# Six merge gates of branch B, in pairs of seven half-width products

## The chip, the core and the metric

The kernel runs on one core of a Trainium2 chip, as one program with one launch. The core has five engines that work side by side, each through its own queue in order: TensorE (PE) multiplies matrices and transposes into PSUM; VectorE (DVE) and ScalarE (ACT) work element by element and read PSUM; GpSimd (POOL) works element by element in SBUF; SyncE (SP) issues nearly all DMA. An engine that waits for a semaphore holds up everything behind it in its queue. The metric is the device time of one execution in microseconds (us), the median of three runs.

## The reference

Two layers of a bidirectional encoder, 512 tokens of width 1024, all in float32:

```python
h = x @ w_in[l]
c_q, c_kv, k_r, gate_a, q_d, k_d, v_d, gate_b, gates = _split_cols(h)
# branch A: latent attention, 8 heads -> y_a (512 wide), y_a = (o_a * silu(gate_a)) @ w_branch_a[l]
# branch B: differential attention, 4 heads, each head's output RMS-normed -> y_b,
#           y_b = (o_b * silu(gate_b)) @ w_branch_b[l]
g = jax.nn.sigmoid(gates + b_merge[l])
merged = g[..., :D_MODEL] * y_a + g[..., D_MODEL:] * y_b
out = merged @ w_out[l]
x = _layer_norm(DEEPNORM_ALPHA * x + out, ln_gamma[l], ln_beta[l])
```

The change is about the second half of `gates`, 1024 columns of `x @ w_in` in 8 chunks of 128 columns (gtB0 to gtB7).

## The kernel before

**Layout and precision.** x stands feature-major in SBUF: 8 chunks of 128 features by 512 tokens. Every float32 operand is split into a high and a low part that PE multiplies at full speed: xH and xL for x, `slot` (L107 to L114) for a weight: one load of 128x1024 into a `wr` tile (2 buffers), one cast on ACT (L110), two subtractions on DVE (L113). A product is three matmuls, high x high, high x low, low x high (`mm3`, L123 to L126). `proj` (L128) makes one chunk of 128 output columns: 8 feature chunks x 3 = 24 matmuls of 512 tokens.

**Stages of a layer.** Latent projections, then branch A's heads, then branch B's four heads, then gates and branch outputs, the merge, the output projection and the LayerNorm. While one head's values are worked out, the next head's scores and other projections are woven in (`dfill`, L567). `diff_values` (L455) of a branch B head: transposes of the probabilities (L179) into PSUM, a cast (L181, ACT) and a low part (L182, DVE) per chunk, 3 value matmuls per chunk, a copy (L467), transposes (L473), squares (L476), two small DVE operations (L478, L479), the power -0.5 on POOL (L481), a broadcast by four transposes (L141) and three DVE operations (L484, L485, L161) that give yB. The last head (3) has no next head beside it. `yB` is needed by `branch(1, c)` (12 matmuls of 512 for one chunk), `yA`, held in 8 `y` tiles, by `branch(0, c)`, whose last call is chunk 7 (m7). After head 3: gate B0, then four times two gates and two branch products, each merged on DVE (L596, L597) and split (L163, L164) into `qm` tiles.

**What sets the order.** The code says what depends on what, in program order, with a number of buffers per tag; a scheduler then sets every engine's queue by its own estimate of when each operand is ready. It may move a matmul of a later projection between two steps of an earlier chain, if its weights are there by its estimate. At run time each queue keeps that order.

Of the kernel before, what the change touches and what calls it, by code (L numbers as in the profile page):

```python
# [11 lines left out]
F32 = mybir.dt.float32  # L12
# [6 lines left out]
DM = 1024  # L19
SEQ = 512  # L20
P = 128
# [21 lines left out]
    + [f"o{n}{k}" for n in range(2) for k in range(4)]  # L43
)

# [5 lines left out]
def hybrid_trunk(ctx: ExitStack, tc: tile.TileContext, x, xT, wlat, wts, prm, dlam, gb, tab, rtab, out):  # L51
# [23 lines left out]
    def pt_(tag):  # L75
        return ps.tile([P, 512], F32, tag=tag, name=nm("ps" + tag), bufs=PB[tag])
# [106 lines left out]
        return h, lo  # L183

    def layer(l, last):
        pr = prms[:, l, :]
        A, B = slice(0, 64), slice(64, 128)

# [266 lines left out]
        def diff_values(h, pts, v, g, s1):  # L455
# [22 lines left out]
            nc.vector.scalar_tensor_tensor(e, s1, EPS_DIFF, s1, ALU.mult, ALU.mult)  # L478
            nc.vector.scalar_tensor_tensor(e, ss, 1.0 / 128, e, ALU.mult, ALU.add)  # L479
            r = small(4)  # L480
            nc.gpsimd.tensor_tensor(r, e, mhalf[:, 0:4], ALU.pow)  # L481
            yield
            b = bcast(r)
            nc.vector.scalar_tensor_tensor(g, b, gsc, g, ALU.mult, ALU.mult)  # L484
# [7 lines left out]
        def branch(which, c, ys):  # L492
            if c % 2 == 0:
                br[which] = slot(l, f"br{'AB'[which]}{c // 2}")
            bhh, bll = br[which]
            acc = pt_("acc")
            for k in range(4):
                o = ((c % 2) * 4 + k) * P
                mm3(acc, bhh[:, o:o + P], bll[:, o:o + P], ys[k][0], ys[k][1], k == 0, k == 3)
            return acc  # L500

        def gate(which, c):
            acc = proj(l, f"gt{'AB'[which]}{c}")
            th = t2("tmp")
            col = which * 8 + c
            nc.scalar.activation(th, acc, AF.Tanh, bias=bh[:, col:col + 1], scale=0.5)
            return th

        mA = []

# [18 lines left out]
                        gens.remove(g)  # L529
            return r  # L530

        qd, kd, vd, gB, hold = {}, {}, {}, {}, {}

        def run(names):
            for f in names:
                i = int(f[-1])
                if f[0] == "a":
                    gateA(i)
                elif f[0] == "g":
                    hold[i] = gate(0, i)  # L540
                elif f[0] == "m":
                    mergeA(i, hold.pop(i))
                elif f[0] == "v":
                    vd[i] = diff_v(i)
                elif f[0] == "b":
                    gB[i] = silu2(proj(l, f"gb{i}"))
                elif f[0] == "q":
                    qd[i] = diff_q(i)
                elif f[0] == "k":
                    kd[i] = diff_k(i)  # L550
# [5 lines left out]
        for h in range(8):  # L556
# [8 lines left out]
            run(fill[h])  # L565
        run(["b0", "v0"])
        dfill = {  # L567
            0: ["g0", "m0", "g1", "m1", "b1", "q2", "k2", "g2", "m2", "g3", "m3"],
            1: ["v1", "b2", "q3", "k3", "g4", "m4", "g5", "m5"],
            2: ["b3", "g6", "m6", "g7", "m7"],  # L570
            3: [],
        }
        s1 = {h: small(4, "s1", 3) for h in range(4)}
# [13 lines left out]
        hold["B0"] = gate(1, 0)  # L587
        next(tail)
        merged = []
        for c2 in range(4):  # L590
            ths = [gate(1, 2 * c2) if c2 else hold.pop("B0"), gate(1, 2 * c2 + 1)]
            for i in range(2):
                c = 2 * c2 + i
                acc = branch(1, c, yB)
                th = ths[i]
                nc.vector.scalar_tensor_tensor(th, th, 1.0, acc, ALU.add, ALU.mult)  # L596
                nc.vector.tensor_tensor(th, th, mA[c // 2][:, i * 512:i * 512 + 512], ALU.add)  # L597
                merged.append(split(th, "qm", 0.5))


        src = x if l == 0 else xs
# [85 lines left out]
def _pack(i, l):  # L687
# [2 lines left out]
    outs = []  # L690
    for s in SLOTS:
        c = int(s[-1]) if s[-1].isdigit() else 0
        if s.startswith("vd"):
            a = _fm(w_in, O_VD + int(s[2]) * 256 + r(256))[:, 4 * c:4 * c + 4]
        elif s[:2] in ("ga", "qd", "kd", "gb"):
# [83 lines left out]
```

## Time and profile before

| | |
|---|---|
| time, median of 3 runs (range) | 855.28 us (854.16 to 855.56) |
| profiled execution | 854.49 us, span 852.7 us |
| PE busy | 841.5 us (99%), 4121 matmuls |
| DVE, ACT, POOL busy | 587.5, 428.8, 22.7 us |
| DMA read from HBM, written | 70.80 MB, 4.19 MB |
| granted PE clock | 0.998 |

In the profile a row of a group reads: line, engine, operation, output<-input by the program's names, shapes, count | busy us, mean ns of one | idle us of the engine just before them, and what ended most of it. A timeline row reads: start us, length us, engine, line, operation, output<-input, shape, count, and in brackets the idle time before it with what ended it. A row of a window reads: stretch, its length, then the busy time and number of instructions of PE, of its weight loads (PEld), DVE, ACT, POOL, then granted clock, DMA share and GB/s. A DMA row reads: output<-input, queue, count, KB each, median us from issue to landing.

### The profile page before, as it was taken

How to read it: one execution, taken by the hardware profiler on the slowest of the kernel's cores; microseconds unless marked ns; L12 is line 12 of the kernel's file. 1: busy time of each engine (PE TensorE's matmuls, PEld its weight loads, DVE VectorE, ACT ScalarE, POOL GpSimd, SP SyncE). 2: the span in 40 equal slices, each digit the busy share in tenths (PEclk: the TensorE clock that was granted, in tenths of full speed). 3: DMA queues.
4: the chain of work that ended last, by engine and by line, in shares of the span. 5: the costliest groups of instructions: out<-in, count | busy, mean ns of one | idle time of the engine just before them, and what ended most of it. 6: DMA issues, size and time to landing. Idle time of an engine off the chain costs nothing.

```text
span 852.7 us, 11036 instructions
## 1 busy us (share of the span) xinstructions
PE 841.5 (99%) x4121; PEld 694.6 (81%) x4121; DVE 587.5 (69%) x1066; ACT 428.8 (50%) x843; POOL 22.7 (3%) x30
## 2 busy tenths in 40 slices
PE   9999999999999999999999999999999999999996
PEld 8777877878898888888897778788788888888885
DVE  6789988586656745455867899877667566545457
ACT  5767775463534633332336777755546354433310
POOL 0100000000000000000120000000000000000001
PEclk9999999999999999999999999999999999999999
DMA  8411111213222352323532110122222233433322
GB/s 295 126 44 33 37 50 50 74 31 102 91 74 75 123 173 83 94 96 118 184 107 69 42 37 26 50 52 73 75 75 75 81 94 123 157 97 94 98 75 98
DMA packets 27701, 75.70 MB, mean 89 GB/s; under 512 B 3200, under 2 KB 7808, under 8 KB 27648
## 3 DMA queue, kind: packets, MB, share of 16 engines
q1 hardware_dynamic: 27648, 75.01, 27.8%
q8 instruction: 32, 0.52, 0.3%
q14 instruction: 21, 0.17, 0.1%
HBM read 70.80 MB, written 4.19 MB: 88 GB/s over the span
## 4 chain that ended last, share of the span: by engine, by line
PE 94%; ACT 3%; DVE 2%; issue 0%; POOL 0%; DVEq 0%
PE psacc L124 23%; PE psacc L125 23%; PE psacc L126 23%; PE pstr L179 4%; PE pspv L362 2%; PE pspv L124 2%; PE pssc L124 2%; PE pssc L125 2%; PE pssc L126 2%; PE pspv L363 2%; PE pspv L125 2%; PE pspv L126 2%; ACT wh L110 1%; PE pssc L441 1%; PE pssc L445 1%; PE pssc L446 1%
## 5 line engine op out<-in xcount | busy, mean ns | idle before, releaser
L113 DVE TENSOR_TENSOR wl<-wr,wh 128x512 fp32r<-128x512 f32 x192 | 127.1, 685 | 146.8 <-ACT wh L110 146.4
L124 PE MATMUL psacc<-xH,wh 128*128 128x512 f32 x512 | 201.6, 394 | 0.0
L125 PE MATMUL psacc<-xL,wh 128*128 128x512 f32 x512 | 200.8, 392 | 0.0
L126 PE MATMUL psacc<-xH,wl 128*128 128x512 f32 x512 | 200.4, 391 | 0.0
L110 ACT CAST wh<-wr 128x1024 fp32r<-128x1024 f32 x96 | 100.8, 1050 | 176.8 <-PE psacc L125 119.0
L124 PEld LDWEIGHTS psacc<-xH,wh 128*128 128x128 f32 x512 | 96.2, 188 | 19.7
L126 PEld LDWEIGHTS psacc<-xH,wl 128*128 128x128 f32 x512 | 96.2, 188 | 19.2
L125 PEld LDWEIGHTS psacc<-xL,wh 128*128 128x128 f32 x512 | 96.2, 188 | 19.2
L172 ACT ACTIVATE p<-pssc,sm 128x512 f32<-128x512 f32 x128 | 88.2, 690 | 27.1 <-DVE sm L170 26.5
L170 DVE TENSOR_REDUCE sm<-pssc 128x1 f32<-128x512 f32 x128 | 86.6, 682 | 5.0 <-PE pssc L126 2.8
L181 ACT CAST pt<-pstr 128x512 fp32r<-128x512 f32 x96 | 55.7, 586 | 28.8 <-PE pstr L179 28.6
L182 DVE TENSOR_TENSOR pt<-pstr,pt 128x512 fp32r<-128x512 f32 x96 | 64.7, 684 | 7.2 <-ACT pt L181 6.3
L179 PE MATMUL pstr<-ident,p 128*128 128x128 f32 x384 | 57.3, 272 | 0.0
L179 PEld LDWEIGHTS pstr<-ident,p 128*128 128x128 f32 x384 | 47.3, 140 | 12.0 <-ACT p L172 0.5
L125 PE MATMUL psacc<-wl,xH 128*128 128x256 f32 x128 | 36.3, 284 | 0.0
L124 PE MATMUL psacc<-wh,xH 128*128 128x256 f32 x128 | 36.3, 284 | 0.0
L126 PE MATMUL psacc<-wh,xL 128*128 128x256 f32 x128 | 36.2, 283 | 0.0
L362 PE MATMUL pspv<-pt,vs 128*128 128x512 f32 x64 | 29.3, 458 | 0.3
L124 PE MATMUL pssc<-kv,qm 128*128 128x512 f32 x64 | 26.8, 423 | 0.5 <-ACT kv L303 0.5
L124 PE MATMUL psacc<-y,wh 128*128 128x512 f32 x64 | 25.8, 403 | 0.0
L363 PE MATMUL pspv<-pt,vs 128*128 128x512 f32 x64 | 25.5, 398 | 0.0
L125 PE MATMUL pssc<-kv,qm 128*128 128x512 f32 x64 | 25.4, 397 | 0.0
(287 smaller groups left out, 1559.0 us busy)
## 6 DMA issues: line engine op xcount, KB each, us to landing
wr<-in_wts_dram SPq DMA_DIRECT2D x106, 512.0 KB, 3.5
p<-in_xT_dram SPq DMA_DIRECT2D x8, 256.0 KB, 5.3
qr<-in_wts_dram SPq DMA_DIRECT2D x16, 128.0 KB, 2.1
p<-in_gb_dram SPq DMA_DIRECT2D x8, 256.0 KB, 3.0
y<-in_x_dram SPq DMA_DIRECT2D x8, 256.0 KB, 5.6
x_scratch<-y SPq DMA_DIRECT2D x8, 256.0 KB, 2.1
y<-x_scratch SPq DMA_DIRECT2D x8, 256.0 KB, 5.0
out_dram<-y SPq DMA_DIRECT2D x8, 256.0 KB, 2.0
```

The lines of the kernel that those rows point to most:

```text
L110: nc.scalar.copy(hi, raw)
L113: nc.vector.tensor_tensor(lo[:, c], raw[:, c], fr(hi[:, c]), ALU.subtract)
L124: nc.tensor.matmul(o, lhsT=lh, rhs=rh, start=start, stop=False)
L125: nc.tensor.matmul(o, lhsT=lh, rhs=rl, start=False, stop=False)
L126: nc.tensor.matmul(o, lhsT=ll, rhs=rh, start=False, stop=stop)
L170: nc.vector.tensor_reduce(m, S, axis=AX.X, op=ALU.max, negate=True)
L172: nc.scalar.activation(p, S, AF.Exp, bias=m, scale=1.0, accum_out=sums)
L179: nc.tensor.transpose(b[:, t * P:(t + 1) * P], pts[t][:, c * P:(c + 1) * P], ident)
L181: nc.scalar.copy(h, b)
L182: nc.vector.tensor_tensor(lo, b, fr(h), ALU.subtract)
L362: nc.tensor.matmul(pv, lhsT=v, rhs=ph, start=kc == 0, stop=False)
L363: nc.tensor.matmul(pv, lhsT=v, rhs=pl, start=False, stop=kc == NT - 1)
```

## The change

Of the 8 gates of branch B in a layer, gtB2 to gtB7 are made as three pairs (`gate_pair`). A pair is a product of a weight of 1024 x 256 and x of 1024 x 512. Each is seen as 2 x 2 blocks: weight blocks of 512 features x 128 columns (r11, r12, r21, r22), x blocks of 512 features x 256 tokens. Instead of 8 block products it makes 7 (a form of Strassen's scheme), each 4 feature chunks x 3 = 12 matmuls of 256 tokens: 84 matmuls where two gates had 48 of 512.

The sums of weight blocks (four adds of 128x512 a pair) are made on POOL (L553) in `kv` tiles; the 7 weight operands are split into high and low parts by ACT and DVE (L558, L559). The raw weights come as four loads of 256 KB into `p` tiles (L548), not through `wr`. The sums of x blocks (`x_forms`, L520) are the same for all pairs of a layer: per j two adds of 128x512 and four of 128x256 on POOL, in `qm` tiles, written to DRAM by two DMAs from POOL's queue; each of the four sums is read back by one load into a `wr` tile and split into four `y` tiles (sums 0 and 1) or `qm` tiles (`load_x_form`, L532). Products add up in three PSUM tiles (Y, Z, X) of half width; between products ACT copies them out (L598 to L606) and DVE adds. The weight blocks and results are the same numbers in another order of sums; rounding differs.

Also changed: the branch products of B use the `sc` PSUM tiles; pairs stand ahead of the branch chunks 0, 2 and 4 in the program; the slots of the weights in DRAM are in another order, with a pair's two gates side by side. The x sums stand in `dfill` behind the power of head 0 (x0, x1) and of head 1 (x2, x3), the read-backs (y0 to y3) behind m7.

```diff
-    + ["gtB0", "gtB1", "brB0", "gtB2", "gtB3", "brB1", "gtB4", "gtB5", "brB2", "gtB6", "gtB7", "brB3"]
+    + ["gtB0", "gtB1", "brB0", "brB1", "brB2", "brB3"] + [f"gtB{c}" for c in range(2, 8)]
...
+        xf = dram.tile([P, 4, 1024], F32, name=f"xf{l}")
...
-            nc.gpsimd.tensor_tensor(r, e, mhalf[:, 0:4], ALU.pow)
+            pows[h] = nc.gpsimd.tensor_tensor(r, e, mhalf[:, 0:4], ALU.pow)
...
-            acc = pt_("acc")
+            acc = pt_("sc" if which else "acc")
...
+        c1, c2 = slice(0, 256), slice(256, 512)
+        XF = []
+        def x_forms(j):
+            ra, rb, f, g = (t2("qm") for _ in range(4))
+            for v, k in ((ra, j), (rb, j + 4)):
+                nc.gpsimd.tensor_tensor(v, fr(xH[:, k, :]), fr(xL[:, k, :]), ALU.add)
+            nc.gpsimd.tensor_tensor(f[:, c1], ra[:, c1], ra[:, c2], ALU.subtract)
+            nc.gpsimd.tensor_tensor(f[:, c2], f[:, c1], rb[:, c2], ALU.add)
+            nc.gpsimd.tensor_tensor(g[:, c1], rb[:, c2], ra[:, c2], ALU.subtract)
+            nc.gpsimd.tensor_tensor(g[:, c2], f[:, c2], rb[:, c1], ALU.subtract)
+            for i, v in ((0, f), (2, g)):
+                nc.gpsimd.dma_start(xf[:, i:i + 2, j * 256:(j + 1) * 256], v.rearrange("p (a b) -> p a b", a=2))
+        def load_x_form(i):
+            raw = load(xf[:, i, :])
+            out = []
+            for o in (0, 512):
+                h, lo = split(raw[:, o:o + 512], "y" if i < 2 else "qm", -1.0 if i == 1 else None)
+                out += [(h[:, c], lo[:, c]) for c in (c1, c2)]
+            XF.append(out)
+        def gate_pair(c):
+            i = SLOTS.index(f"gtB{c}")
+            G = wts[l, i:i + 2].rearrange("s (q r) n -> (s q) (r n)", r=2)
+            raw = []
+            for i in range(4):
+                raw.append(t2("p"))
+                nc.sync.dma_start(raw[i], G[:, i * 512:(i + 1) * 512])
+            r11, r12, r21, r22 = raw
...
+            f3 = add(r11, r21)
+            f1 = add(r21, r22)
+            f2 = add(f3, r22)
+            f4 = add(f2, r12)
+            a, b = halves()
+            W11 = form(r11, a)
+            F1 = form(f1, b)
+            a, b = halves()
+            F2 = form(f2, a)
+            F4 = form(f4, b)
+            F3 = form(f3, two("op"))
+            W12 = form(r12, two("pt"))
+            W22 = form(r22, two("pt"))
...
+            def product(o, w, xs_, first):
+                for k in range(4):
+                    (wh, wl), (h, lo) = (v[:, k * P:(k + 1) * P] for v in w), xs_[k]
+                    for n, (a, b) in enumerate(((wh, h), (wh, lo), (wl, h))):
+                        nc.tensor.matmul(o, lhsT=a, rhs=b, start=first and k == 0 and n == 0,
+                                         stop=k == 3 and n == 2, skip_group_check=True)
+            tag = "g" if c == 4 else "qw"
+            t0, t1 = t2(tag), t2(tag)
+            Y, Z, X = (pt_("acc")[:, c1] for _ in range(3))
+            product(Y, W11, block(0, 0), True)
+            nc.scalar.copy(t0[:, c1], Y)
+            product(Z, F1, XF[0], True)
+            nc.scalar.copy(t1[:, c1], Z)
+            product(Y, F2, XF[1], False)
+            nc.scalar.copy(t0[:, c2], Y)
+            product(Z, F4, block(1, 1), False)
+            nc.vector.tensor_tensor(t0[:, c2], Z, t0[:, c2], ALU.add)
+            product(Y, F3, XF[2], False)
+            nc.scalar.copy(t1[:, c2], Y)
+            product(X, W12, block(1, 0), True)
+            nc.vector.tensor_tensor(t0[:, c1], X, t0[:, c1], ALU.add)
+            nc.vector.tensor_tensor(t1[:, c2], t1[:, c2], t1[:, c1], ALU.add)
+            col = 8 + c
+            nc.scalar.activation(t0, t0, AF.Tanh, bias=bh[:, col:col + 1], scale=0.5)
+            product(Y, W22, XF[3], False)
+            nc.scalar.activation(t1[:, c2], t1[:, c2], AF.Tanh, bias=bh[:, col + 1:col + 2], scale=-0.5)
+            nc.scalar.activation(t1[:, c1], Y, AF.Tanh, bias=bh[:, col + 1:col + 2], scale=-0.5)
+            return t0, t1
...
+                elif f[0] == "x":
+                    with tc.issue_after(pows[max(pows)].ins):
+                        x_forms(i)
+                elif f[0] == "y":
+                    load_x_form(i)
...
-            0: ["g0", "m0", "g1", "m1", "b1", "q2", "k2", "g2", "m2", "g3", "m3"],
-            1: ["v1", "b2", "q3", "k3", "g4", "m4", "g5", "m5"],
-            2: ["b3", "g6", "m6", "g7", "m7"],
+            0: ["x0", "x1", "g0", "m0", "g1", "m1", "b1", "q2", "k2", "g2", "m2", "g3", "m3"],
+            1: ["x2", "x3", "v1", "b2", "q3", "k3", "g4", "m4", "g5", "m5"],
+            2: ["b3", "g6", "m6", "g7", "m7", "y0", "y1", "y2", "y3"],
...
-        for c2 in range(4):
-            ths = [gate(1, 2 * c2) if c2 else hold.pop("B0"), gate(1, 2 * c2 + 1)]
...
+        ths = [hold.pop("B0"), gate(1, 1)]
+        for c in range(8):
+            if c in (0, 2, 4):
+                ths += gate_pair(c + 2)
+            acc = branch(1, c, yB)
```

The order of the queues changes at head 3 of branch B. First PE, in layer 0, around the end of head 3's values. Before, `pspv_3129` are its value matmuls, `psacc_3213` is gate gtB0, L473 its transposes; fourteen more rows of `psacc_3213` follow, then L141 on `pstr_3240`, then gate gtB1:

```order
L124 MATMUL pspv_3129<-pt_3168,kv_2601 128x512
L125 MATMUL pspv_3129<-pt_3169,kv_2601 128x512
L126 MATMUL pspv_3129<-pt_3168,kv_2602 128x512
L124 MATMUL psacc_3213<-xH,wh_3208 128x512
L125 MATMUL psacc_3213<-xL,wh_3208 128x512
L126 MATMUL psacc_3213<-xH,wl_3209 128x512
L124 MATMUL psacc_3213<-xH,wh_3208 128x512
L473 MATMUL pstr_3192<-ident,op_3188 128x128 x4
L125 MATMUL psacc_3213<-xL,wh_3208 128x512
```

And with the change, where `pspv_3218` are the value matmuls, `pstr_3329` is the broadcast of the power (L141) and `psacc_3302` is gtB0:

```order
L141 MATMUL pstr_3264<-ident,sm_3036 128x128 x4
L124 MATMUL pspv_3218<-pt_3257,kv_2650 128x512
L125 MATMUL pspv_3218<-pt_3258,kv_2650 128x512
L126 MATMUL pspv_3218<-pt_3257,kv_2651 128x512
L474 MATMUL pstr_3281<-ident,op_3277 128x128 x4
L141 MATMUL pstr_3329<-ident,sm_3293 128x128 x4
L124 MATMUL psacc_3302<-xH,wh_3297 128x512
L125 MATMUL psacc_3302<-xL,wh_3297 128x512
L126 MATMUL psacc_3302<-xH,wl_3298 128x512
```

The 24 matmuls of gtB0 stood between and behind the steps of head 3's values, all ahead of the last broadcast; now all of them stand behind it, and nothing else stands between the steps.

Second, SP's queue, in layer 0. Before, from gtA6's weights: `wr_3059` is brA3, `wr_3081` gtA7, `wr_3206` gtB0:

```order
L104 DMA wr_3025<-in_wts_dram 128x1024
L104 DMA wr_3059<-in_wts_dram 128x1024
L104 DMA wr_3081<-in_wts_dram 128x1024
L104 DMA wr_3206<-in_wts_dram 128x1024
L610 DMA p_3684<-in_gb_dram 128x512
```

With the change, behind gtA7's weights: the four loads from `xf_90` are the x sums 0 to 3, `p` are blocks of pairs' weights, `wr_3295` is gtB0:

```order
L104 DMA wr_3178<-xf_90 128x1024
L548 DMA p_3373<-in_wts_dram 128x512
L548 DMA p_3375<-in_wts_dram 128x512
L548 DMA p_3377<-in_wts_dram 128x512
L548 DMA p_3379<-in_wts_dram 128x512
L104 DMA wr_3188<-xf_90 128x1024
L548 DMA p_3557<-in_wts_dram 128x512
L104 DMA wr_3198<-xf_90 128x1024
L104 DMA wr_3208<-xf_90 128x1024
L548 DMA p_3559<-in_wts_dram 128x512
L548 DMA p_3561<-in_wts_dram 128x512
L104 DMA wr_3295<-in_wts_dram 128x1024
```

gtB0's weights followed gtA7's at once; now four x sums and seven weight blocks stand ahead of them. `wr_3295` takes the buffer of `wr_3198`, which is free when sum 2 is split.

Third, DVE with the change, behind the squares of head 3 (L480 is the second small operation, L485 the first that reads the broadcast, `wl_3298` the low part of gtB0's weights):

```order
L480 SCALAR_TENSOR_TENSOR sm_3290<-sm_3280,sm_3290 128x4
L161 TENSOR_TENSOR lat_3271<-op_3020,lat_3271 128x512
L485 SCALAR_TENSOR_TENSOR g_3072<-pstr_3329,gs_477,g_3072 128x512
L113 TENSOR_TENSOR wl_3298<-wr_3295,wh_3297 128x512 x2
L486 TENSOR_TENSOR op_3277<-op_3277,g_3072 128x512
```

The low part of gtB0's weights stood ahead of head 3's first L182 in DVE's queue; now it stands behind an operation that reads the broadcast. Layer 1 has the same orders at these places. On POOL the power of head 3 now stands behind five weight adds.

More of the change, by code (lines that the diff above doesn't have):

```diff
@@ new lines, in load_x_form, with add, form, halves @@
+        def load_x_form(i):
[13 more added lines that the diff above has]
+            r11, r12, r21, r22 = raw
+            def add(a, b):
+                o = t2("kv")
+                nc.gpsimd.tensor_tensor(o, a, b, ALU.add)
+                return o
+            def form(v, room):
+                hi, lo = room
+                nc.scalar.copy(hi, v)
+                nc.vector.tensor_tensor(lo, v, fr(hi), ALU.subtract)
+                return room
+            def halves():
+                h, lo = t2("wh", F32R, 1024), t2("wl", F32R, 1024)
+                return [(h[:, o:o + 512], lo[:, o:o + 512]) for o in (0, 512)]
+            def two(tag):
+                return t2(tag, F32R), t2(tag, F32R)
+            f3 = add(r11, r21)
[11 more added lines that the diff above has]
+            W22 = form(r22, two("pt"))
+            def block(i, j):
+                return [(xH[:, 4 * i + k, 256 * j:256 * j + 256], xL[:, 4 * i + k, 256 * j:256 * j + 256])
+                        for k in range(4)]
+            def product(o, w, xs_, first):
[26 more added lines that the diff above has]
+            return t0, t1
@@ L530, in weave @@
             return r
-        qd, kd, vd, gB, hold = {}, {}, {}, {}, {}
+        qd, kd, vd, gB, hold, pows = {}, {}, {}, {}, {}, {}
         def run(names):
@@ L589, in layer @@
         merged = []
-        for c2 in range(4):
-            ths = [gate(1, 2 * c2) if c2 else hold.pop("B0"), gate(1, 2 * c2 + 1)]
[L592 to L598, printed above, removed]
+        ths = [hold.pop("B0"), gate(1, 1)]
[3 more added lines that the diff above has]
+            acc = branch(1, c, yB)
+            th = ths[c]
+            nc.vector.scalar_tensor_tensor(th, th, 1.0, acc, ALU.add, ALU.mult)
+            nc.vector.tensor_tensor(th, th, mA[c // 2][:, (c % 2) * 512:(c % 2) * 512 + 512], ALU.add)
+            merged.append(split(th, "qm", 0.5))
         src = x if l == 0 else xs
@@ L692, in _pack @@
         c = int(s[-1]) if s[-1].isdigit() else 0
+        if s in ("gtB3", "gtB5", "gtB7"):
+            continue
+        if s in ("gtB2", "gtB4", "gtB6"):
+            o = O_GT + DM + c * P
+            a = np.concatenate([_fm(w_in, o + i * P + r(P)).reshape(P, DM) for i in range(2)], 1)
+            outs += list(a.reshape(2, P, 1024))
+            continue
         if s.startswith("vd"):
```

## The prediction

> **What bounds the kernel now.** I read the page's busy table first, then the chain of waits, then the timeline of TensorE (PE) in the places that the diff touches.
>
> ```profile
> span 852.7 us, 11036 instructions
> PE 841.5 (99%) x4121; PEld 694.6 (81%) x4121; DVE 587.5 (69%) x1066; ACT 428.8 (50%) x843; POOL 22.7 (3%) x30
> PE 94%; ACT 3%; DVE 2%; issue 0%; POOL 0%; DVEq 0%
> ```
>
> PE is busy for 99% of the span and holds 94% of the chain that ended last. So a microsecond counts in full when it is taken from PE's stream of matmuls, or when PE is made to wait; work of the other engines counts only when PE waits for it. The busy time of one matmul is no price, since matmuls overlap. The price is the step from one start to the next. Two rows frame the gate and branch stage of layer 0, from the first matmul of the gate projection gtB1 to the first of the output projection:
>
> ```profile
> 320.19 0.47 PE L124 MATMUL psacc<-xH,wh 128*128 128x512 f32 x1
> ...
> 380.15 0.39 PE L124 MATMUL psacc<-wh,qm 128*128 128x512 f32 x1
> ```
>
> Between them lie 7 gates of 24 matmuls and 8 branch products of 12, 264 in all, all 512 columns wide: 59.96/264 = **0.227 us** a matmul, without a hole. The change uses 256 columns; the same form runs in the projection of branch B's values (diff_v):
>
> ```profile
> 152.74 0.28 PE L124 MATMUL psacc<-wh,xH 128*128 128x256 f32 x1
> ...
> 160.90 0.28 PE L126 MATMUL psacc<-wh,xL 128*128 128x256 f32 x1
> ```
>
> 69 rows are 68 steps: 8.16/68 = **0.120 us**. That is more than half of 0.227, so a narrow matmul gives a part of its saving back.
>
> **The change part by part. The products.** A pair was 2 x 24 x 0.227 = 10.88 us; it becomes 7 x 12 = 84 matmuls x 0.120 = 10.08. The gain is 0.80 us a pair and 4.8 us for six pairs. Bounds: half of 0.227 (0.1135, gain 8.1 us) and 0.125 (two steps in the rows round up to it; gain 2.3). I take 0.120, the row of the same form.
>
> **The casts, sums and copies of a pair.** They are to lie beside PE:
>
> ```profile
> L110 ACT CAST wh<-wr 128x1024 fp32r<-128x1024 f32 x96 | 100.8, 1050 | 176.8 <-PE psacc L125 119.0
> L160 ACT CAST qm<-tmp 128x512 fp32r<-128x512 f32 x16 | 9.9, 621 | 2.1 <-DVE tmp L318 1.8
> L229 ACT ACTIVATE qm<-psacc 128x256 f32<-128x256 f32 x6 | 2.3, 387 | 0.0
> L163 ACT ACTIVATE qm<-tmp 128x512 fp32r<-128x512 f32 x16 | 10.1, 632 | 26.3 <-DVE tmp L597 26.3
> L113 DVE TENSOR_TENSOR wl<-wr,wh 128x512 fp32r<-128x512 f32 x192 | 127.1, 685 | 146.8 <-ACT wh L110 146.4
> L312 DVE TENSOR_TENSOR qw<-qr,qw 128x256 fp32r<-128x256 f32 x16 | 6.6, 413 | 2.1 <-ACT qw L311 2.0
> ```
>
> A pair with its two branch products takes PE 10.08 + 24 x 0.227 = 15.5 us. ACT has 7 casts (0.62), four PSUM copies and two tanh of half width (0.39), one full tanh (0.69), two casts of merged (0.63) and one branch cast (1.05): 9.7 us. DVE has 7 low parts (0.69), three half-width adds (0.41), two branch low parts and three operations per merged chunk (0.69): 11.6 us. Both fit. Inside a pair PE waits only where a product reuses a PSUM tile that ACT still has to copy; with one product (1.44 us) between, and at most one cast (0.62) ahead of the copy (0.39) in ACT's queue, I find 0.4 us to spare at the tightest place. Cost: nothing; without this cover a late copy costs up to 0.4 us a product.
>
> **The x sums on GpSimd (POOL).** The trace has no such add. The nearest rows:
>
> ```profile
> masks.py:199 POOL TENSOR_SCALAR_AFFINE_SELECT ident<-ident 128x128 f32<-128x128 f32 x1 | 0.3, 292 | 0.1
> L481 POOL TENSOR_TENSOR sm<-sm,mhalf 128x4 f32<-128x4 f32 x8 | 8.1, 1007 | 577.3 <-DVE sm L479 524.5 <-PE psacc L125 52.7
> wr<-in_wts_dram SPq DMA_DIRECT2D x106, 512.0 KB, 3.5
> y<-x_scratch SPq DMA_DIRECT2D x8, 256.0 KB, 5.0
> ```
>
> For an add of 128x512 the low bound is DVE's 0.69; the high bound is twice (two inputs) four times the 0.292 of 128 columns, 2.3 us. I take 1.2, four times that row. A layer's 8 wide and 16 half-width x adds are then about 20 us of an engine that idles 577 us, issued behind the power (pow) of heads 0 and 1, a whole head ahead of the loads that read them back. Cost: nothing. The four weight adds of a pair (4.8 of 15.5 us) fit too.
>
> **The hole at head 3.** This is the term that decides. wr has two buffers. SP's queue now loads x sums 0 and 1 into them ahead of gtB0's weights, and their splits go into y tiles that hold yA until the last matmuls of branch A's chunk 7. Then sums 2 and 3 take the two buffers, and only then gtB0. So PE has no gate left to put between the steps of head 3's values, as it has now:
>
> ```profile
> 308.53 1.03 PE L179 MATMUL pstr<-ident,p 128*128 128x128 f32 x8
> 310.19 1.28 DVE L182 TENSOR_TENSOR pt<-pstr,pt 128x512 fp32r<-128x512 f32 x2
> 315.05 0.39 PE L126 MATMUL pspv<-pt,kv 128*128 128x512 f32 x1
> 315.48 0.59 ACT L467 COPY op<-pspv 128x512 f32<-128x512 f32 x1 [1.54 <-PE pspv L126]
> 318.08 0.16 DVE L479 SCALAR_TENSOR_TENSOR sm<-sm,sm 128x4 f32<-128x4 f32 x1 [0.44 <-ACT tmp L476]
> 318.33 1.01 POOL L481 TENSOR_TENSOR sm<-sm,mhalf 128x4 f32<-128x4 f32 x1 [25.36 <-DVE sm L479]
> 319.83 0.60 PE L141 MATMUL pstr<-ident,sm 128*128 128x128 f32 x4
> 320.47 0.75 DVE L484 SCALAR_TENSOR_TENSOR g<-pstr,gs,g 128x512 f32<-128x512 f32 x1 [2.23 <-PE pstr L141]
> 308.50:320.20 11.70, 11.65 (x66) 9.29 (x64) 6.94 (x12) 5.88 (x16) 1.01 (x1) 1.00 0.76 244
> ```
>
> The last row is a window, PE first: 11.65 of 11.70 us busy, because gtB0's 24 matmuls (5.44 us) fill it. Count from 308.53. Now gtB1 starts at 11.66, with gtB0 and the broadcast of the power (L141) behind it. In the new order, at the durations above: y0 and y1 are split by 2.0 (DVE), which puts the first low part of the probabilities at 2.1 to 2.7. Sum 2 is issued at 0.2, when y0 is split, and lands at 3.7 (3.5 us); its cast stands in ACT's queue ahead of the third probability cast, which runs 4.35 to 4.9. Casts and low parts of sums 2 and 3 stand between the probabilities' on both engines, so the third low part is done at 5.7 and the fourth at 6.95. The last value matmul ends at 7.7 (now 6.9). Copy, transposes, squares and power take the 3.9 us of now (315.44 to 319.34), the power ending at 11.6; POOL's fifth weight add, ahead of it in the queue, waits for the last value matmul (7.5) and ends at 8.7. L141 runs 11.65 to 12.1. gtB0's buffer is free at 6.35, its weights land at 9.95 and are cast by 11.9, so its first two matmuls follow at once. The third needs the low part, and on DVE that stands behind L484, which needs L141: 12.3 + 0.75 + 0.69 = 13.7. Then 22 x 0.227: **gtB1 starts at 18.7 instead of 11.7, 7.1 us lost in each layer.** Layer 1 has the same order.
>
> Bounds for the hole: with x splits that delay nothing the third probability cast would come 1 us sooner and DVE could be clear, some 4.5 us lost; with sum 2 landing after 5.0 us, as x_scratch does, 8.6. I take 7.1. Behind the hole all of the layer is later; the residual loads, now behind the last pair's products, still fit: 8 x 0.26 MB and the 0.5 MB of weights queued behind them take 10.8 us at the 244 GB/s of that window (its last number), and from there to the output projection lie 4 products, 5.8 us, and 4 branch products, 10.9 us.
>
> **The sum.** The profiled execution took 854.49 us around a span of 852.7, 0.8 under the median. 854.5 - 6 x 0.80 + 2 x 7.1 = 863.9; with the 0.8 to the median 864.7. I say **865**.
>
> **The rivals. The clock falls in the hole** (slower still). PE would do no wide matmul from 7.7 to 13.7 but two. The trace shows a slow start of PE:
>
> ```profile
> L93 PE MATMUL pssc<-p 128*128 128x512 bf16 x9 | 4.0, 628 | 1.2 <-DVE p L90 1.2
> PE pstr L241 <- ACT qm L234: 0.9, 2, 0.5
> ```
>
> The nine warm-up matmuls take (4.02 - 0.63)/8 = 0.42 us a step, about 0.2 above the later 0.227, for 4 us. If the hole brings that state back, nine or so matmuls cost 0.2 more, 2 us a layer: 869. Against it: the hole is broken by transposes, and the longest wait of PE now, but for the start, is 0.5 us (the second row, last number) and cannot tell. [...]
>
> **DVE is slowed by GpSimd.** DVE needs 11.6 of 15.5 us in a pair's stage. If its operations with both inputs in SBUF take double while POOL adds (4.8 us a stage), it needs up to 16.4: 0.9 x 6, and perhaps 1 us in each hole: 872. For it: adds and low parts do fall together. Against it: the trace has no POOL work beside DVE to show it. [...]
>
> **The hole closes** (the other side). If the value chain is as long as it is only because PE was full, it shrinks to PE's own work in it, 11.65 - 5.44 = 6.2 us, and the hole costs nothing: 854.5 - 4.8 + 0.8 = 850.5. It decides as soon as the hole costs under 2.4 us a layer, that is when gtB1 starts before 14.1. For it: PE was full. Against it: the 3.9 us from the last value matmul to the power are ACT, DVE and POOL work that no gate lengthened, and the chain now carries eight x casts and low parts more.
>
> **How the numbers follow.** Forecast 58%, clock 20%, DVE 13%, closed hole 9%. The bounds of the forecast alone (gain 2.3 to 8.1, hole 4.5 to 8.6 a layer) reach from 856 to 870 at their far ends, mostly 860 to 868; with the clock and most of the DVE case the range is 858 to 873. A difference of 0.2% (1.7 us) is what a measurement tells from none: slower 0.89, the same 0.04, faster 0.07.
>
> **What would show it.** Each step has its place in the new profile. The matmuls of the products (L591) step by 0.120 without idle time between products; if not, the PSUM copies are late. PE idles between the last value matmul and gtB0, released by POOL's power, and once more by the low part (L113); gtB1 starts some 18.7 us after head 3's first transposes. If that is under 14, the forecast is wrong; if the first matmuls of gtB0 step by 0.4, the clock fell; if L559 takes well over 0.69 us, POOL slows DVE. The power of head 3 should not wait for the weight adds, nor x sum 0 for its trip through DRAM.

## The result and the profile after

The changed kernel takes **876.09 us** (median; 874.93 to 876.53) against 854.98 for the kernel before on the same chip: a ratio of 1.0246, 95% interval 1.0233 to 1.0258. It is slower, as forecast, but by 21 us and not by 10, and lies outside the range of 858 to 873. The profiled execution took 876.03 us around a span of 874.2. One of the ten executions of run 9 below came in a slow state, 1389.54 us at a granted clock of 0.557; the time given there is that of the other nine. The busy table and chain of the changed kernel:

```profile
span 874.2 us, 11807 instructions
PE 845.9 (97%) x4337; PEld 704.4 (81%) x4337; DVE 638.9 (73%) x1118; ACT 458.5 (52%) x919; POOL 119.5 (14%) x118
PE 87%; DVE 5%; ACT 4%; DMA 2%; issue 1%; POOL 0%; DVEq 0%; SPq 0%; ACTq 0%
```

TensorE (PE) was busy for 99% of the span and holds 97% of it now; VectorE (DVE) and ScalarE (ACT) have come onto the chain. Whom PE waited for, from the table of waits (total us, times, longest). Line numbers are the changed kernel's from here on, one or more higher than before: L474 the transposes of a head's values, L482 the power, L141 its broadcast, L553 a weight sum, L559 the low part of a pair's weight operand, L709 and L710 the merge:

```profile
PE pstr L141 <- POOL sm L482: 6.9, 2, 3.6
PE pspv L125 <- DVE pt L182: 4.4, 6, 1.2
PE pssc L124 <- DVE g L709: 2.0, 2, 1.5
```

None of the three is in the same table of before, where no group but the wait at the start came to more than 0.9 us. The place is the one that the prediction named. PE's timeline at head 3 of layer 0:

```profile
308.90 1.03 PE L179 MATMUL pstr<-ident,p 128*128 128x128 f32 x8
...
315.66 0.50 PE L125 MATMUL pspv<-pt,kv 128*128 128x512 f32 x1 [1.19 <-DVE pt L182]
...
317.68 0.40 PE L126 MATMUL pspv<-pt,kv 128*128 128x512 f32 x1
318.75 0.66 PE L474 MATMUL pstr<-ident,op 128*128 128x128 f32 x4 [0.68 <-ACT op L468]
322.97 1.11 PE L141 MATMUL pstr<-ident,sm 128*128 128x128 f32 x4 [3.57 <-POOL sm L482]
323.74 0.78 PE L124 MATMUL psacc<-xH,wh 128*128 128x512 f32 x1
...
325.53 0.80 PE L126 MATMUL psacc<-xH,wl 128*128 128x512 f32 x1 [0.59 <-DVE wl L113]
326.12 0.63 PE L124 MATMUL psacc<-xH,wh 128*128 128x512 f32 x1
326.55 0.63 PE L125 MATMUL psacc<-xL,wh 128*128 128x512 f32 x1
...
333.15 0.39 PE L124 MATMUL psacc<-xH,wh 128*128 128x512 f32 x1
```

The first row is the zero of the prediction's count (0.37 us later than before), the last is gtB1's first matmul: 24.25 us, against 11.66 before and 18.7 forecast. Three things lie in it. The value chain is longer than the walk had it (the last value matmul ends 9.2 after the zero instead of 7.7, L141 starts at 14.07 instead of 11.65). PE is idle for most of 4.9 us ahead of L141. And then gtB0's matmuls step by 0.43 (326.12 to 326.55) for 0.227, until 331. In layer 1 the same stretch takes 23.52.

Stage by stage, from first-matmul to first-matmul (us), the two layers one after the other:

| stretch | before | changed | forecast |
|---|---|---|---|
| head 3's first transposes to gtB1 | 11.66, 11.65 | 24.25, 23.52 | 18.7 |
| gtB1 to the output projection | 59.96, 59.96 | 57.71, 58.64 | 57.6 |

The first line adds 12.6 + 11.9 us, the second takes 2.3 + 1.3 away; with 0.37 us ahead of layer 0's head 3, near nothing (0.08 us less) between the two stages and 0.3 at the end, these are the 21.5 us between the two spans. So nearly everything that was lost was lost in the hole, 12.2 us a layer where 7.1 was predicted. The question for the experiments is what the other 5 are. The granted clock in windows of 3 us (layer 0, then layer 1; the column behind PE's busy time) and DVE's and GpSimd's (POOL) timeline in the hole name two candidates, the two rivals of the prediction:

```profile
320.00:323.00 3.00, 0.03 (x1) 0.61 0.86 290
323.00:326.00 3.00, 2.41 (x7) 0.50 0.54 166
326.00:329.00 3.00, 3.00 (x8) 0.50 0.67 203
329.00:332.00 3.00, 3.00 (x10) 0.69 0.85 255
...
754.00:757.00 3.00, 2.41 (x7) 0.52 0.46 150
757.00:760.00 3.00, 3.00 (x8) 0.50 0.60 213
760.00:763.00 3.00, 3.00 (x13) 0.84 0.81 227
```

```profile
313.18 2.96 POOL L553 TENSOR_TENSOR kv<-kv,p 128x512 f32<-128x512 f32 x2 [15.24 <-PE pspv L125]
313.47 1.54 DVE L161 TENSOR_TENSOR qm<-wr,qm 128x512 fp32r<-128x512 f32 x1 [1.54 <-ACT qm L160]
314.93 0.68 DVE L182 TENSOR_TENSOR pt<-pstr,pt 128x512 fp32r<-128x512 f32 x1
315.53 1.16 DVE L161 TENSOR_TENSOR qm<-wr,qm 128x512 fp32r<-128x512 f32 x1
317.21 0.68 DVE L161 TENSOR_TENSOR qm<-wr,qm 128x512 fp32r<-128x512 f32 x1
318.26 1.26 POOL L553 TENSOR_TENSOR kv<-p,p 128x512 f32<-128x512 f32 x1 [2.12 <-PE pspv L126]
318.47 1.60 DVE L161 TENSOR_TENSOR qm<-wr,qm 128x512 fp32r<-128x512 f32 x1
```

Counted as either whole or 0.50, the lowest value of a window, the clock is halved for 2 x (0.39 + 0.50 + 0.50 + 0.31) x 3 = 10.2 us in layer 0 and 6.8 in layer 1. And a split of an x sum (L161) takes 1.54 and 1.60 us while POOL adds weights, 0.68 while POOL is silent; in VectorE's queue a probability's low part stands behind the first, and L479 and L480, the small operations ahead of the power, behind the last.

### The profile page after: what moved, and what is told of

Read it like the earlier page. It is cut to its first block, busy times and chain, and to the rows that moved or that the text cites. A ratio compares the mean times of both kernels' runs of the same rounds, so it can differ in the third digit from the quotient of the medians.

```text
span 874.2 us, 11807 instructions
## 1 busy us (share of the span) xinstructions
PE 845.9 (97%) x4337; PEld 704.4 (81%) x4337; DVE 638.9 (73%) x1118; ACT 458.5 (52%) x919; POOL 119.5 (14%) x118
## 4 chain that ended last, share of the span: by engine, by line
PE 87%; DVE 5%; ACT 4%; DMA 2%; issue 1%; POOL 0%; DVEq 0%; SPq 0%; ACTq 0%
PE psacc L124 18%; PE psacc L126 18%; PE psacc L125 18%; PE psacc L591 6%; PE pstr L179 4%; PE pssc L124 3%; PE pssc L125 3%; PE pssc L126 3%; DMA wr<-in_wts_dram 2%; PE pspv L363 2%; PE pspv L124 2%; PE pspv L125 2%; PE pspv L364 2%; PE pspv L126 2%; ACT wh L110 1%; PE pssc L442 1%
## 5 line engine op out<-in xcount | busy, mean ns | idle before, releaser
L124 PE MATMUL psacc<-xH,wh 128*128 128x512 f32 x416 | 166.4, 400 | 0.0
L126 PE MATMUL psacc<-xH,wl 128*128 128x512 f32 x416 | 165.2, 397 | 1.2 <-DVE wl L113 1.2
L125 PE MATMUL psacc<-xL,wh 128*128 128x512 f32 x416 | 165.3, 397 | 0.0
L110 ACT CAST wh<-wr 128x1024 fp32r<-128x1024 f32 x84 | 88.2, 1050 | 116.7 <-PE psacc L125 52.5
L126 PEld LDWEIGHTS psacc<-xH,wl 128*128 128x128 f32 x416 | 79.4, 191 | 18.8 <-DVE wl L113 2.6
L124 PEld LDWEIGHTS psacc<-xH,wh 128*128 128x128 f32 x416 | 79.6, 191 | 16.4
L125 PEld LDWEIGHTS psacc<-xL,wh 128*128 128x128 f32 x416 | 79.5, 191 | 15.9
L482 POOL TENSOR_TENSOR sm<-sm,mhalf 128x4 f32<-128x4 f32 x8 | 9.0, 1130 | 468.0 <-DVE sm L480 468.0
L182 DVE TENSOR_TENSOR pt<-pstr,pt 128x512 fp32r<-128x512 f32 x96 | 64.7, 684 | 4.8 <-ACT pt L181 3.9
L179 PEld LDWEIGHTS pstr<-ident,p 128*128 128x128 f32 x384 | 47.3, 140 | 11.9 <-ACT p L172 0.5
L363 PE MATMUL pspv<-pt,vs 128*128 128x512 f32 x64 | 29.2, 457 | 0.4
L124 PE MATMUL pssc<-kv,qm 128*128 128x512 f32 x64 | 26.8, 423 | 0.7 <-ACT kv L304 0.5
L124 PE MATMUL pssc<-lat,wh 128*128 128x512 f32 x64 | 25.1, 393 | 2.0 <-DVE g L709 2.0
```

Source lines behind the costliest of these rows:

```text
L110: nc.scalar.copy(hi, raw)
L124: nc.tensor.matmul(o, lhsT=lh, rhs=rh, start=start, stop=False)
L125: nc.tensor.matmul(o, lhsT=lh, rhs=rl, start=False, stop=False)
L126: nc.tensor.matmul(o, lhsT=ll, rhs=rh, start=False, stop=stop)
L179: nc.tensor.transpose(b[:, t * P:(t + 1) * P], pts[t][:, c * P:(c + 1) * P], ident)
L182: nc.vector.tensor_tensor(lo, b, fr(h), ALU.subtract)
```

## The experiments

All loads, sums and splits of the changed kernel stay in each, unless the text says otherwise.

**1. gtB0 back in its place.**

```diff
-            2: ["b3", "g6", "m6", "g7", "m7", "y0", "y1", "y2", "y3"],
+            2: ["b3", "g6", "m6", "g7", "m7"],
...
         hold["B0"] = gate(1, 0)
+        run(["y0", "y1", "y2", "y3"])
         next(tail)
```

> The changed kernel with one move: the four read-backs of the x sums are written behind gtB0 (behind its gate in program order) instead of ahead of it, so gtB0's 24 matmuls are back between the steps of head 3's values; pairs, x sums and weight sums stay. Theory A (the loss is the unfilled value chain and what it brings with it: after shows 24.3 us in layer 0 and 23.5 in layer 1 from head 3's first transposes to gtB1's first matmul, against 11.7 before): that stretch comes down to 12 to 15 us (12 if gtB1's weights are in time, up to 15 since they now stand behind the x sums in SP's queue), gtB0 steps by 0.227, and the time is 876.1 - 2 x 9.3 to 2 x 12.2 = 852 to 857. Rival B (the pairs and GpSimd's work cost by themselves, wherever the filler is): the time stays above 865.

863.65 us (861.29 to 865.35), ratio 1.0097 (1.0075 to 1.0119): 12.4 us come back, but not the 19 to 24 expected. The stretch takes 17.29 and 17.10 us. gtB0's 24 matmuls step by 0.23 between the steps of the values, and more than half of the loss is gone; in the rest the power is late. POOL and PE in layer 0:

```profile
323.14 1.26 POOL L553 TENSOR_TENSOR kv<-p,p 128x512 f32<-128x512 f32 x1 [2.56 <-DMA p<-in_wts_dram]
324.37 1.47 POOL L482 TENSOR_TENSOR sm<-sm,mhalf 128x4 f32<-128x4 f32 x1
325.89 0.65 PE L141 MATMUL pstr<-ident,sm 128*128 128x128 f32 x4 [3.40 <-POOL sm L482]
```

The power's input was done at 322.7, but a weight sum that waits for a load stands ahead of it in POOL's queue; the power starts 1.7 us late and takes 1.47 us. Behind that wait the clock falls here too: it is 0.72 in the 6 us from 326.0 and in the 6 from 749.0, that is 2 x 0.28 x 6 = 3.4 us at half rate in each layer. Neither theory had this size: the filler is worth 12 of the 21 us, and what is left needs another cause.

**2. The x part alone.** Plain gates gtB2 to gtB7 instead of pairs; the splits of the x sums are made and nobody reads them.

```diff
-            if c in (0, 2, 4):
-                ths += gate_pair(c + 2)
+            if c < 6:
+                ths.append(gate(1, c + 2))
...
```

> The changed kernel with plain gates gtB2 to gtB7 in place of the pairs: x sums, their trip through DRAM, read-backs and splits stay (nobody reads the splits), no weight sums on GpSimd. Up to the first pair TensorE's order is that of the changed kernel. Theory A (x read-backs ahead of gtB0 make the hole, GpSimd's weight sums only lengthen it): head 3's first transposes to gtB1's first matmul 20 to 22.5 us, gtB0's first matmuls still at about 0.43 a step, the stage behind it back at 59.9, so 855 + 2 x 9.6 = 874. Rival C (the hole is there because GpSimd's adds slow VectorE and delay the power): without weight sums it goes to 18.7 or less, no half-rate matmuls, 869 or less.

877.76 us (2 runs, 876.62 and 878.89), a ratio of 1.0267 (1.0247 to 1.0288): without a single pair and without a weight sum the kernel is as slow as the changed one. The stretch takes 23.49 and 23.94 us, the stage behind it 59.84, as before. So the read-backs make the hole, and rival C falls. The hole is 1 us over what I expected, for a reason of its own: sum 3 landed later here (its first cast began 8.5 us behind the zero in layer 0, 6.8 in the changed kernel), and ACT's copy of the values stood behind its casts; PE's transposes L474 waited 4.4 us for that copy in the two layers, 1.4 in the changed kernel. The clock was down for about 10 us in each layer (0.61 in the 13 us from 319 and from 752), with no weight sum in the kernel.

**3. Without the weight sums.** Left out of the computation: the four sums of a pair's weight blocks; the products use plain blocks.

```diff
-            f3 = add(r11, r21)
-            f1 = add(r21, r22)
-            f2 = add(f3, r22)
-            f4 = add(f2, r12)
+            f3, f1, f2, f4 = r11, r21, r22, r12
```

> The changed kernel without the weight sums (left out of the computation: products use the plain blocks), so GpSimd has nothing but its powers in and behind the hole. If GpSimd's adds slow VectorE's splits (1.2 to 1.6 us in the hole instead of 0.69) and the power (1.42 for 1.01): splits back at 0.69, the stretch from head 3's first transposes to gtB1 shorter by 2 to 2.5 us a layer, the wait of branch products on the merge (2.0 us) gone, time 869 to 871. If VectorE is slow for another cause (the loads landing at the same time): the splits stay above 1 us and the time at 875 to 877.

870.91 us (870.48 and 871.35): 5.2 us less than the changed kernel. The splits are back at 686 ns, the power at 1.02 us, L141 starts 11.99 us behind the zero in layer 0 (14.07 with the sums, 11.65 in the prediction's walk), and the stretch takes 21.44 and 21.89 us. The loads land as before (the x sums in 3.9 us in both, the weight blocks in 3.5 for 3.3), so their landing is not what slows DVE. The waits on the merge fell only from 2.0 to 1.6 us; they have another cause, told below. The clock falls without a slowed split as well, here for 2 x 0.34 x 10 = 6.8 us in each layer:

```profile
319.00:329.00 10.00, 7.67 (x22) 0.66 0.54 172
749.00:759.00 10.00, 8.67 (x25) 0.66 0.54 178
```

**4. The hole filled.** Ten matmuls that nobody reads stand between L474 and L141.

```diff
+            if h == 3:
+                idle = pt_("sc")
+                with tc.issue_after(tr.ins):
+                    for n in range(10):
+                        nc.tensor.matmul(idle, lhsT=xH[:, 0, 0:P], rhs=xH[:, 1, :], start=n == 0, stop=n == 9)
```

> The changed kernel with ten 512-wide matmuls of x that nobody reads added between head 3's transposes L474 and the broadcast of its power L141, in both layers (2.3 us of the 4.9 that TensorE stands there). If the half rate of gtB0 (0.43 a step over 13 to 15 matmuls) is the clock, lowered by idleness: gtB0 steps by 0.227 from its first matmul, L141 takes 0.60 instead of 1.1, gtB1 starts 3 us sooner in each layer, 870. If it comes from late operands or from transfers and GpSimd's work beside it: still 0.43 a step, 876.

868.54 us (868.16 and 868.92): added work makes the kernel 7.5 us faster. In layer 1 the clock stays at 1.00, and gtB0 steps by 0.23 from its second matmul on (the last row is a window with PE's busy time and the clock):

```profile
748.11 2.53 PE L487 MATMUL pssc<-xH 128*128 128x512 f32 x10
751.70 0.65 PE L141 MATMUL pstr<-ident,sm 128*128 128x128 f32 x4 [1.06 <-POOL sm L482]
752.10 0.48 PE L124 MATMUL psacc<-xH,wh 128*128 128x512 f32 x1
...
752.88 0.40 PE L124 MATMUL psacc<-xH,wh 128*128 128x512 f32 x1
753.11 0.39 PE L125 MATMUL psacc<-xL,wh 128*128 128x512 f32 x1
...
753.00:756.00 3.00, 3.00 (x15) 1.00 0.54 109
```

gtB1 starts 19.80 us behind the zero (23.52 without the filling). In layer 0 the clock had fallen at 317.8, ahead of the ten matmuls; they ran at half rate, 4.61 us for 2.53, the clock was back at 324.6, and gtB0 ran at full rate (21.34 for 24.25). So the half rate is the clock's and follows what PE did before; late operands or transfers beside it are not its cause. The last 22 of gtB0's steps take 5.00 us in both layers, for 7.62 and 7.20 in the changed kernel. Part of the gain is not the clock's: gtB0's low part was ready here before PE asked for it, so that its third matmul starts 0.3 and 1.5 us sooner.

**5 to 7. Another order.** The read-backs behind gtB1 and branch chunks 0 and 1, each pair right ahead of its chunks; then pairs 2 and 4 in a row; then that with the residual loads behind the first half of the output weights. The first has the residual loads there too. In all three the weight sums are issued behind head 3's power on POOL.

```diff
-            if c in (0, 2, 4):
-                ths += gate_pair(c + 2)
+            if c == 2:
+                run(["y0", "y1", "y2", "y3"])
+            for p in {2: (2, 4), 4: (6,)}.get(c, ()):
+                ths += gate_pair(p)
...
+            with tc.issue_after(pows[3].ins):
+                f3 = add(r11, r21)
```

> The changed kernel with another order: the four read-backs of the x sums are written behind gtB1 and branch B's chunks 0 and 1, each pair stands right ahead of the two chunks that use it (pairs 2, 4, 6 ahead of chunks 2, 4, 6), every weight sum is issued behind head 3's power on GpSimd, and the residual loads are written behind the first half of the output projection's weights. Theory A (nothing is lost but the hole and its followers): head 3's first transposes to gtB1 11.7 to 13 us as before, no half rate, a pair 9.77 us for 10.88 (six: 6.7 us), so 854.8 + 0.8 (start-up shift of x sums) - 6.7 = 849, up to 854 where merges or weights come late. Rival (ACT and VectorE, now with read-backs, splits and merges in the same stage, become the bound): above 856, with waits of TensorE on VectorE's low parts behind the branches.

> As the run before, but pairs 2 and 4 follow one another ahead of chunk 2, pair 6 stands ahead of chunk 4, and the residual loads stay where the changed kernel has them. Theory A: 849 to 854, with four branch products behind the last pair to cover the residual loads and merges as in the changed kernel. Rival: two pairs in a row (19.5 us) leave VectorE's 14 low parts and GpSimd's 8 sums (8 x 1.4 = 11.2 us) no cover: products wait for the second pair's low parts, above 855.

> As the run before, with the residual loads behind the first half of the output projection's weights. If these loads delay the output projection anywhere, this is faster than the run before by that; theory A expects no difference (under 1 us) where four branch products lie between.

866.02, 863.88 and 862.79 us (2 runs each; before 855.56). The hole is closed in each (12.4 us), and the stage behind it, which could take 56.6 us by the pairs' and branches' own rows (120 x 0.227 + 3 x 9.77), takes 62.8 to 64.8. My theory A fell here: the hole is not all. The timeline of the third of them, with POOL adding without a pause from 320.9 to 331.4:

```profile
323.34 3.00 POOL L553 TENSOR_TENSOR kv<-kv,p 128x512 f32<-128x512 f32 x2
325.12 1.77 DVE L486 TENSOR_TENSOR op<-op,g 128x512 f32<-128x512 f32 x1
326.82 1.79 DVE L559 TENSOR_TENSOR wl<-kv,wh 128x512 fp32r<-128x512 f32 x1
...
333.70 3.43 POOL L553 TENSOR_TENSOR kv<-p,p 128x512 f32<-128x512 f32 x2
334.21 0.67 DVE L712 SCALAR_TENSOR_TENSOR tmp<-tmp,pssc 128x512 f32<-128x512 f32 x1
```

DVE's operations with both inputs in SBUF (L486, L559) take 1.77 and 1.79 us here for 0.69, a factor of 2.6; L712, one of whose inputs lies in PSUM (pssc), takes 0.67 beside such sums. What PE itself waits for in this stage is mostly ACT's copies of the products (in run 7 L599 and L601, 2.7 us each in the two layers) and a low part of head 3 (2.0 us). Taking the residual loads out of the way was worth 1.1 us, where theory A had expected under 1.

**8 to 10. The same sums on VectorE.** Twice in the new order with the later residual loads (pairs in a row, and pairs spread; the weight sums no longer wait for the power), once with the changed kernel's own order and hole.

```diff
-                nc.gpsimd.tensor_tensor(o, a, b, ALU.add)
+                nc.vector.tensor_tensor(o, a, b, ALU.add)
```

> As the run with pairs in a row and later residual loads, but the 12 weight sums of a layer are made by VectorE (0.69 us each by its rows) instead of GpSimd (1.3 to 1.7 us), so GpSimd is silent behind head 3's power. Theory D (VectorE was slowed by GpSimd's sums: its operations with two SBUF inputs took 1.8 us there for 0.69): these rows come back to 0.69, VectorE gains more than the 8.3 us a layer that the sums cost it, TensorE's waits for ACT's copies and VectorE's low parts between the branches (3 to 4 us a layer) go, and the gate and branch stage comes from 63 towards 57 us: 849 to 853, faster than before. Rival (VectorE was simply full): the stage stays at 62 or more, 862 or more.

> As the run ahead of it, with the pairs spread (pair 2 ahead of chunk 2, pair 4 ahead of chunk 3, pair 6 ahead of chunk 4). Theory D: 849 to 853; the branch between pairs 2 and 4 gives ACT and VectorE 2.7 us more, so if they are late with two pairs in a row this is faster by up to 2 us a layer, else the same.

> The changed kernel with one edit: the weight sums are made by VectorE instead of GpSimd; the order, with its hole, stays. Theory D (same sums, other engine; the slowing goes with GpSimd's adds and not with the sums): splits in the hole at 0.69, power at 1.01, head 3's first transposes to gtB1 21 to 22.5 us (without sums 21.4 and 21.9, changed kernel 24.3 and 23.5), 870 to 873. Rival (VectorE full): 876 or more, since 8.3 us a layer are added to it.

The last one keeps everything else of the changed kernel: one word is changed, DVE is given 8.3 us more work a layer, and the kernel falls from 876.09 to 867.46 us (865.71 and 869.21), below what either theory had. The stretch takes 19.82 and 20.12 us, close to the prediction's 18.7, and the stage 56.91 and 56.98. DVE's rows, first of the changed kernel, then of this one:

```profile
L182 DVE TENSOR_TENSOR pt<-pstr,pt 128x512 fp32r<-128x512 f32 x96 | 64.7, 684 | 4.8 <-ACT pt L181 3.9
L161 DVE TENSOR_TENSOR qm<-wr,qm 128x512 fp32r<-128x512 f32 x8 | 9.7, 1213 | 3.1 <-ACT qm L160 3.1
L559 DVE TENSOR_TENSOR op<-kv,op 128x512 fp32r<-128x512 f32 x6 | 6.1, 1010 | 0.2
```

```profile
L182 DVE TENSOR_TENSOR pt<-pstr,pt 128x512 fp32r<-128x512 f32 x96 | 64.7, 684 | 4.7 <-ACT pt L181 3.9
L161 DVE TENSOR_TENSOR qm<-wr,qm 128x512 fp32r<-128x512 f32 x8 | 5.5, 687 | 3.9 <-ACT qm L160 3.9
L559 DVE TENSOR_TENSOR op<-kv,op 128x512 fp32r<-128x512 f32 x6 | 4.1, 687 | 0.2
```

L182 reads PSUM and is the same in both, 684 ns. Here the clock fell too, but for less long:

```profile
320.00:323.00 3.00, 1.38 (x6) 0.67 0.60 214
323.00:326.00 3.00, 3.00 (x12) 0.76 0.54 193
```

That is 2 x (0.33 + 0.24) x 3 = 3.4 us. The profiled executions differ by 10.3 us, in these parts: gtB0's third matmul, the first that needs the low part, starts 2.3 and 2.2 us sooner behind the zero, its last 22 steps take 5.48 and 5.97 us for 7.62 and 7.20, and the stage behind is 2.5 us shorter, mostly the waits on the merge (told below). Only the first is what the sums did to the chain. That the clock was down for a shorter time cannot be put down to them: in run 3, which has no sums and the third matmul within about 0.2 us of the same place, it was down twice as long.

The two in the new order take 854.0 us (ratio 0.9986, 0.9976 to 0.9995) and **853.56 us (0.9984, 0.9974 to 0.9994)**: the best version, 22.5 us under the changed kernel and 1.4 under the kernel before. That is a difference that the interval tells from none, and a small one, below the 0.2% that the prediction called measurable. Run 8 against run 7 shows the price of the sums on GpSimd without the clock: 8.8 us, with a granted clock of 1.00 in layer 0 from 309 to the end of the stage in both, and 0.997 and 0.998 over the whole span. Theory D's mechanism held: all splits and sums took 0.69, PE's waits for L599 and L601 are gone, and the stage came down to 57.4 to 58.5 us. Its sum did not, 854 for 849 to 853: the stretch ahead still takes 13.2 us, since x splits and weight sums stand between DVE's steps towards the power.

**11 and 12. Less work ahead of the power.** In the spread version, all VectorE work of the pairs behind L480, then the splits of the x sums too.

```diff
+                with tc.issue_after(pres[3].ins):
+                    ths += gate_pair(p)
```

> As the spread run with VectorE's sums, but every weight sum and low part of a pair is issued on VectorE behind the last operation ahead of head 3's power (L480), so head 3's chain has only two x splits in it that before has not. Theory E (of that run's 13.2 us from head 3's first transposes to gtB1, 1.5 more than before, the part that the four weight sums and low parts ahead of L480 took comes back): 12.2 to 12.8 us, 852 to 853. Rival (VectorE's work is only pushed into the first pair, whose products then wait for low parts): as fast as that run, 853.6, or slower.

> As the run ahead of it, with VectorE's low parts of the x sums behind L480 too. Theory E: 11.7 to 12.2 us from head 3's first transposes to gtB1, as before, 851 to 852.5. Rival: the x sums' two load buffers are held longer, sums 2 and 3 and the weights of the branches behind them come late, and products or branches wait: 854 or more.

853.86 us (ratio 0.9986, 0.9977 to 0.9996) and 854.23 (0.9992, 0.9983 to 1.0002). The stretch shrinks as theory E says, to 12.5 and 12.0 us, and the time does not: the first pair takes 10.6 to 11.2 us instead of 9.8, and branches wait up to 1.1 us for a cast. The rival held. What is taken from the chain's steps comes back in the stage behind it.

## Why the prediction was right and wrong

**The products: right in kind, too small in size.** They step without idle time. A pair takes 9.77 us from its first matmul to the branch behind it:

```profile
353.84 0.28 PE L591 MATMUL psacc<-xH,wh 128*128 128x256 f32 x1
...
363.61 0.39 PE L124 MATMUL pssc<-lat,wh 128*128 128x512 f32 x1
```

9.77/84 = 0.116 us a step for the 0.120 taken, a gain of 1.1 us a pair for 0.8, inside the bounds. The last pair of a layer takes 9.98, a gain of 0.9, so six pairs give 4 x 1.1 + 2 x 0.9 = 6.2 us.

**The hole: right place, right mechanism, but two of its prices were wrong.** The walk took 0.69 us for each of DVE's operations and 0.227 for each step of gtB0. The first shows in the start of gtB0's third matmul, the first that needs the low part, the second in the 22 steps from there to gtB1. In us, layer 0 and layer 1:

| | third matmul, behind the zero | the last 22 steps |
|---|---|---|
| the walk | 13.7 | 5.0 |
| changed kernel | 16.63, 16.32 | 7.62, 7.20 |
| without weight sums (run 3) | 14.55, 14.28 | 6.89, 7.61 |
| sums on VectorE (run 10) | 14.34, 14.15 | 5.48, 5.97 |
| hole filled (run 4) | 16.34, 14.80 | 5.00, 5.00 |

Run 2 shows the same loss with no pair at all.

**The first step that failed: the weight sums on GpSimd, which "fit too" and were given no cost.** They do fit their engine (1.33 to 1.45 us each by their rows, not 1.2). But the walk priced each of DVE's operations in the hole at 0.69. It counted the engine that adds and not what the sums do to the other engine's operations (1.54 and 1.60 us for 0.68 in the hole of layer 0). By the table they make the third matmul 2.1 and 2.0 us late; leaving them out gave 5.2 us in all (run 3). The prediction had this as a rival at 13%, with a price of 7.4 us: 0.9 x 6 in the stages of the pairs and 2 for the holes. The doubling behind the 0.9 was the author's supposition and no run shows it as such; the operations with both inputs in SBUF that began beside an add took 1.15 to 1.65 us for 0.69 in the changed kernel. There the loss lay the other way round, 4.1 us in the holes and 0.4 in the stage behind (57.71 and 58.64 for 58.02 and 57.90 in run 3); only in the new order did it lie in the stages of the pairs (run 7 against run 8). The chance was too low and the place was wrong. "The trace has no POOL work beside DVE to show it" was said against it, and the absence of a case is no evidence against the mechanism.

**The second step that failed: gtB0's last 22 matmuls at 0.227 a step.** The clock fell, as the 20% rival said. By the table that costs 7.62 + 7.20 - 2 x 5.0 = 4.8 us; the rival's price of 4 us (0.2 us over nine or so matmuls in each layer, rounded up) was near.

**The two were priced as alternatives.** Forecast, clock and slowed DVE together make 865 + 4 + 7.4 = 876.4, and 876.1 was measured, but the parts fit less well than the sum. Against the forecast the runs show 4.1 us for the sums in the holes, 1.4 that the walk was too short even without them (run 3), 4.8 for the clock and 2.0 for waits on the merge, less 1.4 that the products gave beyond their 4.8: 10.9 of the 11.1 us. That the two rivals' prices meet the measured time is luck, that both came true is not: each was given a time alone, and the range ended at the dearest single one. Whether the slowed splits also made the clock stay down longer is not shown. It was down for 10.2 and 6.8 us in the changed kernel and 3.4 in each layer of run 10, but also for 6.8 in each layer of run 3 and about 10 in each layer of run 2, which have no weight sums.

**A smaller failure: the residual loads, which "still fit".** They land in time for the projection, but the projection's first weights stand behind them in SP's queue, and VectorE meets those weights' low part ahead of a merge (L709) that a branch waits for. ACT, DVE and PE of the changed kernel, layer 0:

```profile
382.86 1.05 ACT L110 CAST wh<-wr 128x1024 fp32r<-128x1024 f32 x1 [3.05 <-DMA wr<-in_wts_dram]
```

```profile
383.94 0.69 DVE L113 TENSOR_TENSOR wl<-wr,wh 128x512 fp32r<-128x512 f32 x1 [5.67 <-ACT wh L110]
384.55 0.68 DVE L709 SCALAR_TENSOR_TENSOR g<-g,pssc 128x512 f32<-128x512 f32 x1
```

```profile
385.29 0.50 PE L124 MATMUL pssc<-lat,wh 128*128 128x512 f32 x1 [0.56 <-DVE g L709]
```

The last four branches took 11.8 and 12.7 us where 10.9 were counted; 2.0 us of that are these waits. Run 10 has the same order of the queues; its cast came 12.9 us behind the last pair's first matmul for 13.8 here, and no branch waited. The prediction asked whether the loads land before the projection, not who else stands behind their users in a queue.

**What held:** the x sums, at 26 us of GpSimd a layer for the 20 counted, stand a whole head ahead, and TensorE reaches head 3 of layer 0 only 0.37 us later. In the changed kernel the power of head 3 did not wait for weight sums (its input L480 was done at 321.4, it began at 321.5), though it does once the order moves (run 1). The closed hole, the rival on the other side, is out: the hole costs 12 us a layer.

## What to carry to other kernels

Work moved to an idle engine is free only if it takes nothing from the busy ones: ask which operands it reads and which engine reads from the same memory at that time (here DVE's operations with both inputs in SBUF took up to 1.79 us for 0.69 beside GpSimd's sums, one with an input in PSUM 0.67). Where a stage loses the filler of a dependency chain, count every engine's work that slips in between the chain's steps, and then ask whether the resulting idleness lowers TensorE's clock, as it did in the changed kernel with 3.57 and 3.34 us of idle time ahead of L141 and in run 10 with 2.9. And when two rivals can happen together, the sum of their prices belongs in the range.

## What the runs showed of the hardware

- GpSimd's add of two 128x512 fp32 tiles took 1.26 to 1.84 us (changed kernel, run 1). A DVE operation of the same shape with both inputs in SBUF that began beside such an add took 1.15 to 1.65 us in the changed kernel and 0.99 to 1.79 in run 7, for 0.69; with an input in PSUM it stayed at 0.67 to 0.68 (L712 in run 7, L182 in the changed kernel). The same sum on DVE itself took 0.69, so in run 7 handing it over cost DVE more than doing it: its busy time was 648.0 us with the sums on GpSimd (run 7) and 645.3 with them on DVE (run 8). In the changed kernel's own order it was the other way round, 638.9 and 645.3 (run 10).
- TensorE's half clock came in stretches of 10.2, 6.8 and 3.4 us (layers 0 and 1 of the changed kernel, each layer of run 10; 6.8 in each layer of run 3, 3.4 in each of run 1), while steps of wide matmuls took 0.43 for 0.227 us. All are multiples of 3.4; why, no run shows. In layer 1 of the changed kernel the clock fell only at the end of an idle stretch of 3.3 us (1.00 from 751 to 754, 0.52 from 754 to 757), in layer 0 within one of 3.6 that lasts to 322.97 (0.61 from 320 to 323), so in these two the time since the idleness began did not alone decide. Full idleness is not needed: in layer 0 of run 4 it fell at 317.8, where PE had been busy for 2.3 of the 4 us from 314 to 318 and its longest idle time was 1.27 us. What makes it fall stays open.
- Ten matmuls that nobody reads, put into TensorE's idle stretch, made a kernel 7.5 us faster (run 4).
